# Folding 768 columns on TensorE in the tail of a 2D prefix-sum kernel

## Chip, cores and metric

One core of one Trainium2 chip. The metric is the device time of an execution in microseconds (us); lower is better. "Same" means within 2%. A run over 1.5% above the fastest of its kernel would be called slow.

## The reference

```python
B, H, W = 4, 4224, 4224                     # x: float32
ps   = np.cumsum(np.cumsum(x, axis=1), axis=2)
diag = np.diagonal(ps, axis1=1, axis2=2)    # ps[b, i, i]
return np.cumsum(diag, axis=1)              # (4, 4224)
```

All of x has to be read once, 285 MB; the output is tiny.

## The kernel before

The kernel streams x in strips of 384 rows. ScalarE and VectorE sum rows, TensorE adds strips into the diagonal accumulator d. The last strip of the last batch is cut into pieces so that little work is left when the last load lands: "part a" (256 rows) in a first piece, columns 1536 to 3839, and a second piece, columns 0 to 1535; then "part b" (128 rows) in five small pieces. Row sums of part a are split over two engines and collected in `asum`; `arows` adds them up; TensorE then weighs `arows` and part b's sums (`fin_a`, `fin_b`, `fin_e`), and VectorE adds the carry and writes the result.

The code is shortened; `...` marks what is left out.

```python
def act_sum(acc, src):      # ScalarE: copy in place, accumulate
    nc.scalar.activation(out=src, in_=src, func=ACT.Copy, accum_out=acc)
def row_sums(acc, src):     # VectorE
    nc.vector.reduce_sum(out=acc, in_=src, axis=AX.X)
def pair_sum(acc, src):     # VectorE: left half + right half, accumulate
    ...
asum = last.tile([P, 2, 5], FP32, name="asum")
... # the main stream of strips
acuts = [(1536, NH), (0, 1536)]          # part a: first piece, second piece
for c0, c1 in acuts:
    load(out=part_a[:, :, c0:c1], in_=src_a[:, :, c0:c1])
... # five loads of part b
def sum_a(k, c0, c1, ca):
    for h in range(2):
        act_sum(asum[:, h, k : k + 1], part_a[:, h, c0:ca])
    for h in range(2):
        pair_sum(asum[:, h, k + 1 : k + 2], part_a[:, h, ca:c1])
...
matmul(carry_ps, earlier, pu, start=True)
matmul(carry_ps[:, 1:2], apart, pu[:, 0:1])
sum_a(1, *acuts[0], acuts[0][0] + 1216)  # first piece
... # carry copy, two scans, outputs of the other batches
sum_a(3, *acuts[1], acuts[1][0] + 640)   # second piece
row_sums(arows, asum)
weigh_b(dtot[:, 2:3], weights, M0, start=True)
... # fin_a, fin_b of arows; sums of part b; fin_b, fin_e; final adds
```

## Time and profile before

| | before |
|---|---|
| median of 3 runs | 671.47 us (671.45 to 672.24) |
| span of the profiled run | 669.7 us |
| DMA | 285.61 MB at 426 GB/s |
| VectorE / ScalarE / TensorE busy | 67% / 40% / 12% |
| first piece of part a lands | 657.3 us |
| second piece lands | 661.1 us |
| closing products (first `fin_a` to last `fin_b`) | 662.96 to 667.14, at half clock |
| last add (`ye`) begins | 667.56 us |

In the profile, PE is TensorE, PEld its weight loads, DVE VectorE and ACT ScalarE. The square bracket at the end of a timeline line is how long the engine sat idle before the group and what ended that. The profile calls the identity `ones_all`, after the tile in which it lies. To compare runs whose loads shift by a few tenths, I give times from the landing of the second piece of part a, which is when both engines begin its sums.

### The profile page before, as it was taken

The numbers are of one execution on the slowest core, as the hardware profiler recorded it, in microseconds if no ns is written. First come the engines' busy times: TensorE is split into PE (matmuls) and PEld (weight loads), VectorE is DVE, ScalarE is ACT, GpSimd is POOL, SyncE is SP. The second block draws the span as 40 slices with busy tenths as digits, with TensorE's granted clock in tenths as the row PEclk, the third lists the DMA queues.
The fourth block names the chain that finished last, engine by engine and source line by source line (L and its number), as shares of the span: only waits on it lengthen the run. The fifth ranks groups of instructions, "written<-read, shape, count | busy, mean of one in ns | idle before, by whom it ended". The sixth has DMA issues, their size and how long they took to land.

```text
span 669.7 us, 1134 instructions
## 1 busy us (share of the span) xinstructions
PE 82.4 (12%) x168; PEld 15.6 (2%) x168; DVE 449.8 (67%) x286; ACT 265.6 (40%) x251; POOL 36.1 (5%) x83
## 2 busy tenths in 40 slices
PE   0000100000010110000011000000002011000083
PEld 0000000000000000000000000000000000000022
DVE  3779766544388877655437988765442999876555
ACT  0013344556602333445661223344566122334744
POOL 5000000000000000000000000000000000000020
PEclk9999999999999999999999999999999655555577
DMA  9999999999999999999999999999999999999996
GB/s 374 436 436 436 436 436 436 433 436 427 433 424 424 427 436 436 436 436 436 433 436 433 433 436 430 436 418 430 424 436 436 436 436 436 436 436 411 427 420 266
DMA packets 8155, 285.61 MB, mean 426 GB/s; under 512 B 904, under 2 KB 1332, under 8 KB 1876
## 3 DMA queue, kind: packets, MB, share of 16 engines
q0 software_dynamic: 7680, 284.89, 98.7%
q1 hardware_dynamic: 468, 0.66, 0.3%
q14 instruction: 6, 0.05, 0.0%
q8 instruction: 1, 0.02, 0.0%
HBM read 285.47 MB, written 0.07 MB: 426 GB/s over the span
## 4 chain that ended last, share of the span: by engine, by line
DMA 66%; ACT 16%; DVE 13%; issue 2%; PE 1%; POOL 0%; ACTq 0%; DVEq 0%; POOLq 0%
DMA strip<-in_x_dram 66%; ACT strip L211 16%; DVE u L231 5%; DVE u L303 3%; DVE strip L300 2%; DVE above L214 2%; DVE sums L214 1%; PE d L205 0%; PE fin_b L205 0%; DVE c L385 0%; PE fin_a L205 0%; POOL strip L347 0%; ACTq L211 0%; DVE pu L214 0%; DVE c L234 0%
## 5 line engine op out<-in xcount | busy, mean ns | idle before, releaser
L211 ACT ACTIVATE strip<-strip 128x768 f32<-128x768 f32 (+14 forms) x125 | 260.1, 2081 | 399.8 <-DMA strip<-in_x_dram 374.2
L231 DVE TENSOR_TENSOR u<-u,strip 128x3840 f32<-128x3840 f32 (+10 forms) x115 | 292.2, 2541 | 2.7
L300 DVE TENSOR_TENSOR strip<-strip,um 128x1152 f32<-128x1152 f32 x41 | 55.7, 1358 | 184.2 <-ACT strip L211 184.0
L205 PE MATMUL d<-u,sel 128*33 128x384 f32 (+1 forms) x88 | 64.6, 845 | 575.8 <-DVE u L231 575.8
L214 DVE TENSOR_REDUCE above<-strip 128x3 f32<-128x1152 f32 x41 | 55.5, 1353 | 1.4
L292 POOL DMA_DIRECT2D strip<-in_x_dram x38 | 20.2, 531 | 560.3 <-DVE u L231 504.2
L211 ACT ACTIVATION_READ_ACCUMULATOR strip<-strip 128x1 f32 x125 | 23.3, 186 | 0.0
L205 PEld LDWEIGHTS d<-u,sel 128*33 128x33 f32 (+1 forms) x88 | 8.0, 136 | 630.0 <-DVE u L231 627.0
L303 DVE TENSOR_TENSOR u<-strip 128x4224 f32<-128x4224 f32 x4 | 18.2, 4549 | 0.0
L220 DVE SCALAR_TENSOR_TENSOR pair<-strip 128x640 f32<-128x640 f32 (+6 forms) x15 | 10.2, 679 | 9.0 <-DMA strip<-in_x_dram 8.9
L205 PE MATMUL d<-strip,sel 128*11 128x384 f32 x30 | 10.0, 486 | 0.5 <-DVE strip L234 0.5
L214 DVE TENSOR_REDUCE sums<-strip 128x3 f32<-128x1152 f32 x4 | 5.4, 1341 | 6.0 <-DMA strip<-in_x_dram 6.0
L198 DVE TENSOR_SCALAR steps<-steps 128x128 int32<-128x128 int32 x1 | 0.2, 226 | 7.0 <-POOL steps L197 7.0
L322 POOL DMA_DIRECT2D strip<-in_x_dram x6 | 3.1, 528 | 27.4 <-issue 27.4
L214 DVE TENSOR_REDUCE pu<-d 33x1 f32<-33x384 f32 (+1 forms) x2 | 1.1, 548 | 3.6 <-PE d L205 3.6
L234 DVE SCALAR_TENSOR_TENSOR strip<-strip,um 128x384 f32<-128x384 f32 x6 | 3.3, 558 | 0.2
L358 POOL DMA_DIRECT2D strip<-in_x_dram x5 | 2.7, 553 | 4.9 <-DMA strip<-in_x_dram 4.9
L205 PEld LDWEIGHTS d<-strip,sel 128*11 128x11 f32 x30 | 2.7, 93 | 7.7 <-issue 6.0
L205 PE MATMUL d<-ones_all,r 128*33 128x128 f32 (+1 forms) x12 | 2.3, 348 | 0.1
L205 PE MATMUL fin_a<-weights,arows 128*1 128x256 f32 (+1 forms) x4 | 1.4, 513 | 6.1 <-DVE arows L214 6.1
L347 POOL DMA_DIRECT2D strip<-in_x_dram x2 | 1.4, 709 | 13.2 <-issue 13.2
L205 PE MATMUL fin_b<-weights,bsum 128*1 128x128 f32 (+2 forms) x12 | 2.1, 362 | 0.0
(70 smaller groups left out, 34.2 us busy)
## 6 DMA issues: line engine op xcount, KB each, us to landing
strip<-in_x_dram POOLq DMA_DIRECT2D x41, 6336.0 KB, 28.0
strip<-in_x_dram POOLq DMA_DIRECT2D x6, 2112.0 KB, 22.3
strip<-in_x_dram POOLq DMA_DIRECT2D x1, 2304.0 KB, 18.9
strip<-in_x_dram POOLq DMA_DIRECT2D x1, 1536.0 KB, 22.0
strip<-in_x_dram POOLq DMA_DIRECT2D x3, 480.0 KB, 23.1
head<-in_x_dram SPq DMA_DIRECT2D x1, 576.0 KB, 4.1
strip<-in_x_dram POOLq DMA_DIRECT2D x1, 352.0 KB, 23.8
strip<-in_x_dram POOLq DMA_DIRECT2D x1, 128.0 KB, 19.3
```

Source lines behind the costliest of these rows:

```text
L205: nc.tensor.matmul(o, lhsT=lhsT, rhs=rhs, start=start, stop=False, skip_group_check=True)
L211: nc.scalar.activation(out=src, in_=src, func=ACT.Copy, accum_out=acc)
L214: nc.vector.reduce_sum(out=acc, in_=src, axis=AX.X)
L220: nc.vector.scalar_tensor_tensor(out=pair[:, :w], in0=src[:, :w], scalar=1.0, in1=src[:, w:], op0=ALU.mult, op1=ALU.add, accum_out=acc,)
L231: nc.vector.tensor_add(out=o, in0=o, in1=i)
L234: nc.vector.scalar_tensor_tensor(out=o, in0=i, scalar=1.0, in1=m, op0=ALU.mult, op1=ALU.mult, accum_out=acc,)
L292: load(out=strip, in_=rows_of(b, g))
L300: nc.vector.tensor_mul(out=block, in0=block, in1=um3)
L303: nc.vector.tensor_add(out=u, in0=strip[:, 0, :], in1=strip[:, 1, :])
L322: load(out=strip[:, q, :], in_=rows_of(b, g)[:, q, :])
L347: load(out=part_a[:, :, c0:c1], in_=src_a[:, :, c0:c1])
L358: load(out=part_b[:, sb, c0:c1], in_=x[b, r0 : r0 + R, :NH].rearrange("r (k c) -> r k c", k=4)[:, :, c0:c1],)
```

## The change

The intent is to use the nearly idle TensorE: three fp32 products with the identity add three blocks of 256 columns (of both row blocks) on top of each other in PSUM, so ScalarE and VectorE have 768 columns fewer to sum in the first piece. In return VectorE reduces the 2 x 256 columns that remain.

```diff
-    asum = last.tile([P, 2, 5], FP32, name="asum")
+    asum = last.tile([P, 2, 6], FP32, name="asum")
@@
+            c0, c1 = acuts[0]
+            cp = c0 + 768
+            fold_a = psum_s.tile([P, 2, 256], FP32, name="fold_a")
@@
-            sum_a(1, *acuts[0], acuts[0][0] + 1216)
+            sum_a(1, cp, c1, cp + 768)
+            for c in range(c0, cp, 256):
+                matmul(fold_a, ident, part_a[:, :, c : c + 256], start=c == c0)
@@
         sum_a(3, *acuts[1], acuts[1][0] + 640)
+        row_sums(asum[:, :, 5], fold_a)
```

## The prediction

> **What bounds the kernel now.** I read the page first (parts 2 and 4), then the chain of work that ended last in order of time, then the timeline of the last 15 us, then stretches of that end with the granted clock. Part 2 of the page, the DMA row and the TensorE clock row:
>
> ```profile
> PEclk9999999999999999999999999999999655555577
> DMA  9999999999999999999999999999999999999996
> ```
>
> The DMA engines are at 90% or more in 39 of 40 slices: 285.61 MB at 426 GB/s. The change leaves every load as it was, so about 660 of the 669.7 us cannot move. What can move lies between the landing of part a's first piece (657.3 us) and the last output. The chain of waits, in order of time:
>
> ```profile
> 639.12 21.96 DMA strip<-in_x_dram
> 661.08 0.02 issue
> 661.11 1.56 ACT strip L211 x4
> ...
> 662.74 0.17 DVE arows L214
> ...
> 662.96 1.44 PE fin_a L205 x4
> 664.40 2.76 PE fin_b L205 x16
> ...
> 667.18 0.29 DVE yl L424
> ...
> 667.56 0.18 DVE ye L457
> ```
>
> So the end is not set by the sums of the first piece. It is set by the second piece's landing (661.11), its ScalarE sums, the small reduction arows, and then 4.20 us of TensorE (1.44 + 2.76) without a gap. The timeline shows what each engine waited for around it:
>
> ```profile
> 657.32 0.72 DVE L220 SCALAR_TENSOR_TENSOR pair<-strip 128x544 f32<-128x544 f32 x1 [1.12 <-DMA strip<-in_x_dram]
> 657.40 1.22 ACT L211 ACTIVATE strip<-strip 128x1216 f32<-128x1216 f32 x1 [3.56 <-DMA strip<-in_x_dram]
> 661.11 0.74 ACT L211 ACTIVATE strip<-strip 128x640 f32<-128x640 f32 x1 [1.20 <-DMA strip<-in_x_dram]
> 661.11 0.63 DVE L220 SCALAR_TENSOR_TENSOR pair<-strip 128x448 f32<-128x448 f32 x1 [0.15 <-DMA strip<-in_x_dram]
> 662.74 0.16 DVE L214 TENSOR_REDUCE arows<-asum 128x2 f32<-128x10 f32 x1 [0.33 <-ACT strip L211]
> 666.36 0.29 DVE L220 SCALAR_TENSOR_TENSOR pair<-strip 128x128 f32<-128x128 f32 x1 [0.25 <-DMA strip<-in_x_dram]
> 667.18 0.28 DVE L424 TENSOR_TENSOR yl<-fin_b,c 1x128 f32<-1x128 f32 x1 [0.52 <-PE fin_b L205]
> ```
>
> ScalarE is already idle for 1.20 us and VectorE for 0.15 us when the second piece lands: the work that the change takes off them has no reader waiting for it. Near the end, VectorE sits idle until each piece of part b lands, and the last wait (0.52 us) is for TensorE. The last load, seen at 666.36, gives a floor not far below the present end. The stretches with the granted clock (columns: the stretch, its length, busy us and count of PE, PEld, DVE, ACT and POOL, then the granted TensorE clock as a share of full speed, the DMA share and GB/s):
>
> ```profile
> 656.50:660.00 3.50, 0.39 (x6) 0.09 (x2) 2.58 (x7) 2.51 (x4) 0.00 (x0) 1.00 1.02 416
> 660.20:663.50 3.30, 0.54 (x2) 0.21 (x3) 2.54 (x8) 2.08 (x6) 0.00 (x0) 0.50 0.99 392
> 663.50:666.90 3.40, 3.40 (x20) 2.12 (x18) 1.91 (x9) 1.82 (x6) 0.00 (x0) 0.50 0.12 44
> 666.90:667.50 0.60, 0.41 (x9) 0.28 (x6) 0.28 (x1) 0.00 (x0) 0.00 (x0) 0.94 0.00 0
> ```
>
> The closing 4.2 us of TensorE ran at half clock. The clock fell near 660.1, some 3.2 us after the last matmuls (656.9), and came back near 666.95.
>
> **What the Trainium skill says.** "TensorE: Matmul & The Clock Gate", Part 1 (the HAM clock gate), says that the array clock is 2.4 or 1.2 GHz, chosen by activity in free-running windows of about 3.4 us. This trace agrees: full clock from 643.05, half from about 660.1, full from about 666.95, which are 5 and 2 windows of 3.41 us apart. "FP8 and Floating Point Precision", TensorE Precision Notes, says true fp32 takes four passes. The trace agrees: at full clock a 384-column fp32 product takes two instructions of 0.328 us, and 4 x 384 / 2.4 GHz is 0.64 us. "VectorE: DVE Perf Modes", Mode 1x, says fp32 reads from PSUM go one element a cycle; the 384-wide reduction pu<-d took 0.55 us, which is 0.40 at 0.96 GHz and 0.15 of fixed cost.
>
> **The change part by part.**
>
> Removed from ScalarE: two sums of 1216 columns become 768. From 1.22 and 1.20 us each they fall by 448 / 1.2 GHz = 0.37, so 0.75 us in all, all of it in front of a wait for the second piece (1.20 us becomes about 1.95). Worth nothing.
>
> Removed from VectorE: two pair sums of 544 become 384, 160 / 0.96 GHz = 0.17 each, 0.33 in all, in front of the carry copy, the scans and the wait for the second piece (0.15 becomes about 0.48). The scans' readers (the outputs and the final adds) are not waiting. Worth nothing unless the second piece lands early.
>
> Added on TensorE: three fp32 products of 512 columns with the identity. At full clock each is 4 x 512 / 2.4 = 0.85 us, 2.6 us in all with the weight loads mostly hidden; I allow 2.8. They begin at about 657.35, while the clock is still full, and end near 660.1. If cold they would take 5.1 us and end at 662.5. The product for dtot that now stands at 656.51 moves behind them and ends near 660.4; nobody waits for it. The fold has an accumulator of its own.
>
> Added on VectorE: one reduction of 512 fp32 elements from PSUM: 0.53 + 0.15 = 0.68 us. In program order it stands behind the pair sums of the second piece (over at 662.41) and in front of arows: 662.43 to 663.11. VectorE would have idled there for 0.33 us, until ScalarE's 662.66. So arows begins near 663.05 and not at 662.74: +0.31 us on the path that sets the end, and TensorE's closing work begins near 663.27 and not at 662.96.
>
> Behind that VectorE has slack to absorb the rest: the first pair sum of part b runs 0.45 us later, the second 0.26 later, and the last two still begin when their data land (665.73 and 666.36).
>
> Moved: the clock state of the closing products. With no other effect they end 0.31 us later, 667.46 instead of 667.15, or a little less as the clock returns near 666.95 and some 0.5 us of them is left for full clock. If the fold keeps the clock full, 4.2 us becomes about 2.1 to 2.6: part a's products are over by 664.7, part b's follow their data, and the end is set by the last load: pair sum 666.36 to 666.66, two small products to about 666.95, the final add near 667.05 instead of 667.56. That is -0.5 us.
>
> Which state holds depends on the phase of the windows. The fold ends near 660.2 to 660.4 and the closing work starts near 663.3: an idle gap of 2.9 to 3.1 us, a little less than one window, so no window is wholly idle. But this trace shows that a window with about 0.2 us of work (656.7 to 660.1) still led to half clock, while one with 2.0 us (653.3 to 656.7) did not. With the phase of this trace the window 660.1 to 663.5 would hold about 0.5 us, too close to call. Over all phases I put it near half and half. Expected: 0.5 x (-0.5) + 0.5 x (+0.25) = -0.1 us, on 671.47: 671.4.
>
> **The rivals.**
>
> First, the fold keeps the clock full and the end falls to the floor of the last load: 671.0. For it: the gap is now under one window. Against: the phase of this trace puts almost all of the gap into one window.
>
> Second, the new reduction in front of arows is a new wait, and the clock is half anyway: 671.7 to 671.8. For it: VectorE executes in order, and its idle time there was only 0.33 us.
>
> Third, relief of ScalarE and VectorE shortens the end, as the intent may have been: with the first piece's 0.75 and 0.33 us taken off the path, 670.7 or less. Against it: both waited for the second piece already.
>
> Fourth, the fold starts cold and late, so that its reduction waits until 662.6 or later and pushes everything: up to 672.3. Against: 9.2 us of dense products end at 653, with further ones up to 656.9, and the clock reads 1.00 up to 660.
>
> **Range and chances.** The rivals span 670.7 to 672.3, which is 0.2% of the time; 2% would be 13.4 us, more than everything that comes after the landing of the first piece. Three runs of before spread by 0.8 us without any change, which is more than the effect. Predicted 671.4, range 670.8 to 672.1. Faster by over 2%: 0.005; within 2%: 0.99; slower: 0.005.
>
> **What would show the steps right or wrong.** In the timeline after: six fold instructions of about 0.43 us from 657.35; ScalarE idle some 1.9 us before the second piece; a PSUM reduction of about 0.68 us between the pair sums and arows, with no wait for TensorE in front of it; arows at about 663.05; the granted clock 0.5 or 1.0 from there, and the closing products accordingly 4.2 or under 2.7 us long. If the clock stays full, the last add should follow the last landing (ScalarE or VectorE's part of esum) and no longer the fin_b products. The prediction is wrong if the first piece lands at another time, if loads or their landings slow down while TensorE reads the strip, if the reduction takes far more than 0.7 us, or if the end moves by more than 1 us.

## The result and the profile after

The changed kernel took 671.23 us (median of 4 runs, 670.92 to 671.95); the kernel before, 671.67 us (4 runs, 671.45 to 672.24). The ratio of the fast runs is 0.9994, 95% interval 0.9976 to 1.0011: the same. A ratio is the mean time of one kernel's fast runs over that of the other's of the same rounds, so not quite the ratio of the medians.

The chain that ended last, changed kernel, in order of time (start, us, what):

```profile
661.01 0.64 DVE pair L220 x2
...
661.68 0.63 DVE pair L220 x2
662.31 0.62 DVE asum L214
...
663.05 0.18 DVE arows L214
...
663.27 1.34 PE fin_a L205 x4
664.62 2.58 PE fin_b L205 x16
...
667.60 0.18 DVE ye L465
```

Compare it with the chain in the prediction. The 1.56 us of ScalarE have gone from the path. VectorE's two pair sums and the new reduction, which writes `asum`, have taken their place. The timeline of the same kernel around the change:

```profile
657.24 2.84 PE L205 MATMUL fold_a<-strip,ones_all 128*128 128x512 f32 x6 [0.76 <-DMA strip<-in_x_dram]
661.01 0.74 ACT L211 ACTIVATE strip<-strip 128x640 f32<-128x640 f32 x1 [1.95 <-DMA strip<-in_x_dram]
661.01 0.62 DVE L220 SCALAR_TENSOR_TENSOR pair<-strip 128x448 f32<-128x448 f32 x1 [0.49 <-DMA strip<-in_x_dram]
662.23 0.69 DVE L214 TENSOR_REDUCE asum<-fold_a 128x2 f32<-128x512 f32 x1
663.27 1.34 PE L205 MATMUL fin_a<-weights,arows 128*1 128x256 f32 x4 [2.88 <-DVE arows L214]
```

The work taken off the engines has become waiting for the second piece: ScalarE's idle time grew from 1.20 to 1.95 us, VectorE's from 0.15 to 0.49. The reduction takes 0.69 us. `arows` starts 2.04 us after the second piece has landed and not 1.63. The stretches of the changed kernel, cut where the clock changes and one window earlier (columns: stretch, length, busy us and count of PE, PEld, DVE, ACT, POOL, granted clock, DMA share, GB/s):

```profile
656.59:660.00 3.41, 2.76 (x6) 1.06 (x6) 2.67 (x7) 1.76 (x4) 0.00 (x0) 1.00 1.02 417
660.00:663.41 3.41, 0.54 (x4) 0.17 (x4) 2.76 (x8) 2.08 (x6) 0.00 (x0) 1.00 0.99 393
663.41:666.82 3.41, 3.41 (x17) 1.98 (x16) 2.07 (x11) 1.82 (x6) 0.00 (x0) 0.50 0.15 59
```

The fold kept the clock full through 660 to 663.41, where it did little good, and the clock fell just as the closing products began. In this profiled execution (671.49 us) the last add begins 6.59 us after the second piece lands, 0.14 later than before (6.45): slightly slower. Two other executions of the same kernel took 670.92 and 670.96 us. The experiments have to explain both.

### The profile page after: what moved, and what is told of

Its sections match the earlier page's. It is cut to its first block, busy times and chain, and to the rows that moved or that the text cites. A ratio compares the mean times of both kernels' runs of the same rounds, so it can differ in the third digit from the quotient of the medians.

```text
span 669.8 us, 1147 instructions
## 1 busy us (share of the span) xinstructions
PE 84.9 (13%) x174; PEld 16.4 (2%) x174; DVE 450.1 (67%) x287; ACT 264.9 (40%) x251; POOL 36.1 (5%) x83
## 2 busy tenths in 40 slices
DMA packets 8155, 285.61 MB, mean 426 GB/s; under 512 B 904, under 2 KB 1332, under 8 KB 1876
## 4 chain that ended last, share of the span: by engine, by line
DMA 66%; ACT 16%; DVE 14%; issue 2%; PE 1%; POOL 0%; ACTq 0%; DVEq 0%; POOLq 0%
DMA strip<-in_x_dram 66%; ACT strip L211 16%; DVE u L231 5%; DVE u L303 3%; DVE strip L300 2%; DVE above L214 2%; DVE sums L214 1%; PE d L205 0%; PE fin_b L205 0%; DVE c L392 0%; PE fin_a L205 0%; DVE pair L220 0%; POOL strip L347 0%; ACTq L211 0%; DVE asum L214 0%
## 5 line engine op out<-in xcount | busy, mean ns | idle before, releaser
L211 ACT ACTIVATE strip<-strip 128x768 f32<-128x768 f32 (+13 forms) x125 | 259.3, 2075 | 400.4 <-DMA strip<-in_x_dram 374.8
L205 PE MATMUL fold_a<-strip,ones_all 128*128 128x512 f32 x6 | 2.8, 610 | 0.8 <-DMA strip<-in_x_dram 0.8
L392 DVE TENSOR_TENSOR_SCAN c<-ones_all,carry,c 33x384 f32<-33x384 f32 (+1 forms) x2 | 2.0, 1008 | 0.1
```

Of the source, the lines that this page charges most:

```text
L205: nc.tensor.matmul(o, lhsT=lhsT, rhs=rhs, start=start, stop=False, skip_group_check=True)
L392: nc.vector.tensor_tensor_scan(out=c12[:, i, :], data0=ones_row[:rows], data1=src, initial=carry[:, i : i + 1], op0=ALU.mult, op1=ALU.add,)
```

## Experiments

Twelve kernels ran, counting four repeats, in three groups of four; each group shared one chip (a different one each time) and its own runs of the kernel before. All of those runs and the first four together are 31 runs of the kernel before, median 671.45 us, 671.02 to 672.68.

Theory A: the relief lies in front of a wait and is worth nothing; the new reduction delays `arows`; whether the closing products run at full or half clock decides a further half us. Rivals: the relief shortens the end; the fold disturbs loads or engines; the clock doesn't matter.

### 1. The relief alone

The changed kernel without these lines, and without those that only they need:

```diff
-            for c in range(c0, cp, 256):
-                matmul(fold_a, ident, part_a[:, :, c : c + 256], start=c == c0)
-        row_sums(asum[:, :, 5], fold_a)
```

> The changed kernel without the fold and without its reduction: ScalarE sums 768 columns and VectorE 384 pairs, and 768 columns are left out, so the result is wrong on purpose. Theory A (the relief lies in front of a wait for the second piece): ScalarE idles 1.9 to 2.0 us and VectorE 0.5 us before the second piece, arows begins 1.6 us after that landing as before, and the time is that of before within 0.3 us. Rival (the relief shortens the end by 0.3 to 0.75 us): 670.9 or less in fast runs of the same clock.

671.22 us against 671.45, ratio 0.9992 (0.9980 to 1.0005). The comparison with the reference passed although 768 columns are missing, so it says nothing about the exactness of these sums. Timeline:

```profile
661.05 0.74 ACT L211 ACTIVATE strip<-strip 128x640 f32<-128x640 f32 x1 [1.94 <-DMA strip<-in_x_dram]
662.68 0.17 DVE L214 TENSOR_REDUCE arows<-asum 128x2 f32<-128x10 f32 x1 [0.34 <-ACT strip L211]
```

`arows` stands 1.63 us after the second piece, exactly as before; the last add begins after 6.48 us (before: 6.45). In this trace the relief is worth nothing on the path. The median is lower by 0.23, inside the interval. The five runs go from 670.63 to 671.57; 670.63 is the lowest of all runs here, it has no trace, and why it is so low is not shown.

### 2. The fold alone

The kernel before, plus three such products (of the last 768 columns of the first piece), read by nobody.

> The kernel before plus the three fold products, which nobody reads (right result). Theory A: arows begins 1.6 us after the second piece lands, 0.3 earlier than in the changed kernel; the closing TensorE work is either about 4.2 us (half clock, end as before) or under 2.8 us (full clock, end 0.4 to 0.5 us earlier), and no load is later. In the phase of the two traces so far the window from 660.1 to 663.5 then holds about 0.8 us of products, which tells where the threshold is. Rival (the fold's reads of the strip slow the loads or the other engines): pieces of part b land later, or the sums beside it take longer than 1.22 and 0.72 us.

670.95 us, ratio 0.9995 (0.9982 to 1.0008); three runs at 670.93 to 670.95 and two late ones, 671.82 and 672.02, which were not profiled. The sums beside the fold took 1.22 and 0.72 us as before and part b's loads landed as before, counted from the second piece, so in this trace the fold disturbs nothing. The fold itself took longer than planned, in one line of the timeline, and the stretches tell why:

```profile
657.28 4.25 PE L205 MATMUL fold_a<-strip,ones_all 128*128 128x512 f32 x6 [0.75 <-DMA strip<-in_x_dram]
```

```profile
655.17:658.58 3.41, 1.53 (x7) 0.84 (x8) 2.27 (x6) 1.24 (x3) 0.00 (x0) 1.00 1.01 416
658.58:661.99 3.41, 3.41 (x6) 0.76 (x4) 3.15 (x8) 2.21 (x6) 0.00 (x0) 0.50 1.03 416
```

Here the windows stand elsewhere. The one from 655.17 to 658.58 was busy for only 1.53 of 3.41 us, so the clock fell in the middle of the fold. The slow fold then filled the next window completely, and the clock was back at 661.99, before the closing products. The last add begins 5.88 us after the second piece: 0.57 us earlier than before.

### 3. The reduction alone

The kernel before, plus `row_sums(asum[:, :, 5], fold_a)` on a PSUM bank set to zero at the start.

> The kernel before plus the reduction of 512 PSUM elements in front of arows, of a bank set to zero at the start (right result, no fold). Theory A: the reduction takes 0.69 us, arows begins about 2.03 us after the second piece lands and not 1.63 (+0.3 to 0.4), the clock falls to half at the same place as before, and the end is 0.0 to 0.4 us later than before: 671.6 to 671.9. Rival (VectorE had room for it): no change of arows.

671.33 us, ratio 0.9998 (0.9985 to 1.0012). Timeline:

```profile
662.27 0.69 DVE L214 TENSOR_REDUCE asum<-fold_a 128x2 f32<-128x512 f32 x1
663.09 0.17 DVE L214 TENSOR_REDUCE arows<-asum 128x2 f32<-128x12 f32 x1
```

`arows` is at 2.04 us, later by 0.41, as in the changed kernel: the delay is the reduction's. The later end that was expected (671.6 to 671.9) is missed: the median is not higher. In the profiled run the clock happened to come back at 666.11, and the last add began after 6.28 us, 0.17 less than before, so there the clock's place outweighs the reduction. The other four runs have no trace.

### 4. Keeping TensorE busy, without any fold

```diff
+            warm = psum_s.tile([P, GW], FP32, name="warm")
+            for i in range(8):
+                matmul(warm, ident, ones_all[:, P:], start=i == 0)
             sum_a(1, *acuts[0], acuts[0][0] + 1216)
```

> The kernel before plus eight products of constants with 384 columns on TensorE between the carry products and the closing ones, read by nobody (right result). Theory A (the clock in the closing work is the only other thing at stake): TensorE is busy from about 656.4 to 661.7, the granted clock stays 1.0 to the end in every run, the closing work is under 2.8 us, the last add follows the last landing by 0.7 us and not by 1.2, and the time is 0.4 to 0.6 us below before: about 671.0, with a smaller spread. Rival (the closing work is not bound by the clock): same end, 671.4 or more; if the fill delays the closing work, later still.

670.98 us, five runs within 670.90 to 671.08. The same kernel was run again in the third group:

> The kernel before with eight products of constants once more, for the interval. Theory A: granted clock full from the fill to the end, 670.9 to 671.1 in nearly all runs, some 0.4 to 0.6 us below the fast runs of before. Rival: its first five runs were luck, and it spreads as before does, up to 672.

670.93 us: four runs from 670.83 to 670.94 and one of 671.46. The ratios are 0.9990 (0.9977 to 1.0002) and 0.9990 (0.9977 to 1.0004), so by the intervals, which late runs of the kernel before widen, the gain is not proven; 7 of the 10 runs are below the lowest of 31 runs of the kernel before. Timeline of the first:

```profile
656.54 5.43 PE L205 MATMUL warm<-ones_all 128*128 128x384 f32 x16
662.99 0.81 PE L205 MATMUL fin_a<-weights,arows 128*1 128x256 f32 x4 [0.71 <-DVE arows L214]
666.97 0.18 DVE L460 TENSOR_TENSOR ye<-fin_e,yl 1x32 f32<-1x32 f32 x1
```

`fin_a` takes 0.81 us and not 1.44, and its products wait for part b's sums and no longer the other way round. The last add begins 5.84 us after the second piece. Nothing of part a's sums was changed: the clock alone is worth about 0.6 us in the trace and 0.5 to 0.7 in the medians.

### 5. The changed kernel again

> The changed kernel once more, for the spread over clock states. Theory A, as the first runs have sharpened it (the windows of the clock stand at a different place in each run, and a window that is less than about half busy ends in half clock): runs whose mean granted clock is about 0.997 or 0.996 (half clock for one window only, in the middle of the fold, full clock for the closing products) take 670.9 to 671.0, those in which the closing products run at half clock 671.4 to 671.6, apart from runs that are late for another reason. The reduction in front of arows is there in all of them: arows 2.04 us after the second piece lands. Rival (the time doesn't depend on the clock): no order of the times by the clock.

671.58 us against 671.35, ratio 1.0003 (0.9989 to 1.0016). By mean granted clock: 1.000: 671.21; 0.996: 671.18; 0.908: 671.58, 671.59, 672.26. The order by clock is as expected, the level of the faster two is 0.2 us above it; experiment 6 shows that this mean can't sort the runs. The first of them is the profiled run. It had full clock through the fold and the closing products (windows counted back in steps of 3.41 us from 669.30, where the clock falls):

```profile
655.65:659.06 3.41, 1.72 (x8) 0.94 (x9) 2.22 (x9) 1.43 (x3) 0.00 (x0) 1.00 1.02 419
659.06:662.47 3.41, 1.67 (x6) 0.37 (x4) 2.85 (x5) 1.46 (x5) 0.00 (x0) 1.00 1.02 408
662.47:665.89 3.42, 2.29 (x20) 1.43 (x20) 2.61 (x11) 2.25 (x9) 0.00 (x0) 1.00 0.38 146
```

Its fold took 2.84 us and left a gap of 2.88 us, both as in the first trace after the change. But here the gap is split between two windows, which were busy for 1.67 and 2.29 us, and the clock stayed full. Its whole tail, loads included, lay 0.34 us later than in the first trace; the last add still came 5.82 us after the second piece. So two executions with different clocks end with different remainders, and loads that land late hide the difference in the total.

### 6. Two looks at the changed kernel

> One look at the changed kernel for its clock state. Theory A: where the trace shows half clock in the closing products, they take about 4 us and the end is 1.0 us or more behind the last landing; where half clock falls into the fold, the fold takes 3.5 to 4.3 us, ends by 661.6, delays nothing, and the closing products run at full clock.

> The same look a second time: either of the two states, or full clock throughout as in the profile of the repeated run.

Both show the fast close, 670.97 and 671.00 us. In the first, the fold took 4.38 us; its stretches and the end of its chain are:

```profile
653.60:657.02 3.42, 1.69 (x12) 0.65 (x10) 1.38 (x5) 0.23 (x2) 0.00 (x0) 1.00 0.99 411
657.02:660.43 3.41, 3.12 (x4) 1.50 (x5) 3.03 (x7) 1.76 (x4) 0.00 (x0) 0.50 1.03 422
660.43:663.84 3.41, 2.06 (x8) 0.50 (x7) 2.71 (x10) 2.41 (x7) 0.00 (x0) 1.00 0.91 359
```

```profile
666.32 0.31 DVE pair L220 x2
...
666.68 0.23 PE fin_e L205 x2
...
666.94 0.18 DVE ye L465
```

The half clock hit the fold, which ended at 661.69, 0.6 us before its reduction began. The closing products ran at full clock, and the path at the end is now the last landing, its pair sum and two tiny products. `arows` is still at 2.04 us, but nobody waits for it at the end: 5.85 us to the last add. The mean clock alone does not sort the runs: this one has 0.908 like the slow profiled run, because most of that mean is an earlier stretch (about 523 to 643 us) recorded at half clock. In the second look, with 0.997, that stretch is recorded at 1.00, although each matmul of 384 columns up to 642 us took 0.81 to 0.85 us in both looks (0.49 from 644 us on, at full clock). So the two means differ in what was recorded, not in how fast TensorE was, and the place of the last stretch has to be read in the trace. The expectation of experiment 5, which sorted by the mean, was too simple; its order by clock shows nothing.

### 7. The reduction on ScalarE

```diff
-        row_sums(asum[:, :, 5], fold_a)
+        for h in range(2):
+            act_sum(asum[:, h, 5:6], fold_a[:, h, :])
         sum_a(3, *acuts[1], acuts[1][0] + 640)
```

> The changed kernel with the reduction of the fold's result moved from VectorE to two sums on ScalarE, in front of the second piece, where ScalarE was idle for 1.95 us (right result). Theory A: two sums of 256 columns of about 0.4 us end before or just after the second piece lands where the fold ran at full clock, arows begins 1.63 us after that landing as in the kernel before, and the closing products start 0.3 us earlier than in the changed kernel; the time is then 670.9 to 671.0 with full clock and 671.4 with half clock. Where the fold itself is hit by half clock it ends at about 661.5, ScalarE waits for it, and arows is later by 0.5 to 1 us. Rival (the place of the reduction doesn't matter): arows at 2.04 us as in the changed kernel.

671.25 us (670.98 to 672.93), ratio 1.0001 (0.9988 to 1.0013). The two sums of 0.37 us fit in ScalarE's idle time, and `arows` is back at 1.63 us. The last add came after 5.88 us, with full clock in that run (670.98, as expected for it; the median is 0.25 us above that, and the other runs have no trace). The place of the reduction matters for `arows`, and hardly for the end when the clock is full. One run of 672.93 was not profiled and stays unexplained.

### 8. The reduction six times

> The changed kernel with the reduction of the fold's result done six times in a row (right result). Theory A (it lies on the path that sets the end): arows is later by five times 0.62 to 0.69 us, 3.1 to 3.4 us, and so is the end, since nothing behind it has slack of more than 0.3 us: 674.2 to 674.8. Part b's pair sums, in order behind it, add nothing much as their data have landed by then, or up to 1 us where they no longer wait: at most 675.5. Rival (VectorE had room): 671.4 to 672.

That kernel was built on experiment 3 (the kernel before plus reductions) and not on the changed kernel: 675.89 us, above the 675.5 that was to be the most, and `arows` at 6.04 us. So the changed kernel itself was run so too:

> The changed kernel itself with its PSUM reduction done six times (the earlier run of that name was by mistake built on the kernel before with the reduction, without fold). Theory A: arows about 6.0 us after the second piece lands and not 2.04, as in that run, and the time 675.2 to 676.0, so that one reduction is worth about 0.8 us once VectorE is the only bound. Rival (with the fold there is room for it): under 673.

675.49 us (4 runs), ratio 1.0060 (1.0046 to 1.0074). Its timeline:

```profile
663.40 4.32 DVE L214 TENSOR_REDUCE asum<-fold_a 128x2 f32<-128x512 f32 x6
667.86 0.17 DVE L214 TENSOR_REDUCE arows<-asum 128x2 f32<-128x12 f32 x1
```

The second piece landed at 662.18 here, so `arows` is at 5.68 us (about 6.0 was expected), 3.64 later than with one reduction, 0.73 each. The last add came after 10.53 us with the closing products at half clock, 3.94 later than in the first trace after the change, also at half clock: 0.79 each. The time rose by 4.3 us against the changed kernel's 671.21 (median of its eleven runs, on three chips and with the clock in several places), 0.86 each. VectorE in front of `arows` has no room; the single reduction is cheap only because it is short.

### 9. The changed kernel with the clock kept full

One product of constants ahead of the fold, three behind it.

> The changed kernel plus four products of constants on TensorE, one ahead of the fold and three behind it, read by nobody (right result). Theory A: the clock is full from the fold to the end in every run, the closing products take under 2.8 us of their own, and although arows is as late as in the changed kernel (2.04 us after the second piece), the end follows the last landing: 670.9 to 671.1 with a spread under 0.3 us, the same as the kernel before with the fill alone. Rival (the reduction costs its 0.3 to 0.4 us at any clock): 671.3.

670.97 us; four runs from 670.91 to 671.06, one of 671.49; ratio 0.9994 (0.9981 to 1.0006). `arows` is at 2.04 us, the last add at 5.87. With full clock the closing products have slack, and the reduction's 0.41 us disappears in it. The changed kernel then equals the kernel before with the same trick (670.93 to 670.98): the fold adds nothing of its own.

## Why the prediction was right or wrong

| kernel, profiled run | `arows` | last add | clock in the closing products |
|---|---|---|---|
| before | 1.63 | 6.45 | half |
| changed, first trace | 2.04 | 6.59 | half |
| relief alone | 1.63 | 6.48 | half |
| reduction alone | 2.04 | 6.28 | half, full from 666.11 |
| fold alone | 1.64 | 5.88 | full |
| before + fill | 1.64 | 5.84 | full |
| changed again | 2.03 | 5.82 | full |
| changed, two looks | 2.04, 2.04 | 5.85, 5.87 | full |
| changed + fill | 2.04 | 5.87 | full |
| changed, reduction on ScalarE | 1.63 | 5.88 | full |

(us after the landing of the second piece.)

The predicted time and range held: 671.4 was said, 671.23 measured, and the class was the same. That the number came so near is partly luck: it is the mean of two cases, and the four runs happened to split two and two (670.92 and 670.96; 671.49 and 671.95). The next five had a median of 671.58, and the kernel before spreads by 1.7 us. Step by step:

- That loads bound the kernel and only the tail can move: right. Loads, 285.61 MB at 426 GB/s, are the same after.
- The relief is worth nothing: right, by the trace of experiment 1. ScalarE's idle time of 1.95 us and VectorE's of 0.49 were predicted as 1.95 and 0.48.
- The fold takes 2.8 us from full clock: right where the clock stayed full (2.84), and each product pair is as predicted.
- The reduction takes 0.68 us and moves `arows` to 663.05: 0.69 and 663.05. But the second piece landed 0.10 us earlier in that trace, so the delay is 0.41 us and not 0.31. I had let `arows` begin before the reduction was over; it begins 0.13 us after it (662.92 to 663.05), as it reads the reduction's result. The first two pair sums of part b, said to be 0.45 and 0.26 us later, are 0.41 and 0.12 later, counted from the landing.
- The end 0.5 us earlier with full clock and 0.25 later with half clock: right in size. For the changed kernel the last add begins after 5.82 to 5.87 us with full clock and after 6.59 with half clock; before it was 6.45, so 0.58 to 0.63 earlier or 0.14 later.
- "If the fold keeps the clock full": this happened (experiments 5 and 7), but the mechanism was incomplete. I thought that the clock falls after a nearly idle window and that a gap under one window might save it. What differed between the traces was how the windows cut the gap. In the first trace after the change one window held nearly all of the gap of 2.88 us (busy 0.54 of 3.41 us), and the clock fell for the closing products; in experiment 5 the same gap was split between two windows, and the clock stayed full. The prediction also took a slow fold only as a delay. In experiment 2 and in the two looks a window that ended shortly before or during the fold was busy for 1.53, 1.69 and 1.36 us, so a partly busy window was enough; the clock fell there, the slow fold filled the next window, and the closing products ran fast. Busy time alone gives no sharp limit: the window of 1.69 us ended in half clock, those of 1.67 us (experiment 5) and 1.59 us (experiment 7, 658.87 to 662.28) did not.
- The fourth rival (a fold at half clock pushes everything later, up to 672.3) had the wrong sign: it ended at 661.69 and its reduction began at 662.31, and those were the fast executions. The rival assumed a wait that the second piece's sums already covered.
- Half and half for the clock: among eleven runs of the changed kernel, the four with a trace show one slow close and three fast ones, and the other seven are not settled, since their mean clock is ambiguous. The share stays open.
- Most runs that are late by 0.5 to 1.9 us (672.02 in experiment 2, 672.93 in experiment 7, 671.49 in experiment 9) have no trace; late loads are a guess and not shown for them. One late run has a trace, the profiled one of `after_x6` in experiment 8 (676.56 us, 1.0 to 1.3 above the others): there the second piece landed at 662.18 us, 0.7 to 1.2 later than in every other trace.

So the gain did not come from the sums, which was the intent. What the fold can give is TensorE activity shortly before the closing products, and whether that helps depends on where the windows of the clock happen to stand.

## What to carry to other kernels

Before moving work off an engine, look at what that engine does next: if it waits for a load, the relief only lengthens the wait, and whatever the relief costs on the other side may land on the path. A short latency chain on TensorE at the end of a kernel can be worth keeping fast: filling its idle time just before with products that nobody reads gave 0.5 us or so here, more reliably than the useful work did (9 of 10 runs at 671.08 us or less, against 4 of 11 of the changed kernel). When single runs of one kernel differ by as much as the effect, time the steps from a common event in the trace, such as a landing, and compare those.

## What the Trainium skill lacked or had wrong

- "TensorE: Matmul & The Clock Gate", Part 1, tells of a fall to half clock after an idle window and of full clock after a busy one, without a share. Here windows busy (by the profile's modelled ends) for 0.54, 1.36 and 1.53 of 3.41 us (16 to 45%) ended in half clock, and windows of 2.00 and 2.06 us (59 and 60%) did not. In between it is not sharp: one of 1.69 us did (first look), and ones of 1.59 and 1.67 us did not (experiments 7 and 5). From half clock, a window of 2.61 us (76%, experiment 1) did not bring full clock back, one of 2.80 us (82%, experiment 3) did. The window of 3.41 us itself agrees with the traces.
- The same page gives a weight load as its columns over 1.2 GHz, which is 107 ns for 128. Here each fp32 load of the 128-column identity took 186 to 190 ns at full clock and up to 338 ns at half clock; in the fold it was hidden behind the products.
- The same page advises against idle gaps in TensorE for throughput. No page says that products which nobody reads can speed a short closing chain; they did (last add 5.84 us after the second piece and not 6.45).
